# The mixers of a second transformer block: TensorE's order written in the source, long convolution and linear attention interleaved with column projections

## The chip, the cores and the metric

One core of one Trainium2 chip runs the whole program, a network of several blocks, in one launch. The metric is the device time of an execution in microseconds (us). TensorE (PE) multiplies matrices, VectorE (DVE) and ScalarE (ACT) work element by element, SyncE (SP) issues transfers; each engine takes its instructions from a queue of its own, in order, and instructions of different engines wait for each other by semaphores.

## What is computed

The change concerns the four mixers of the second block. The input of the block is normalised, multiplied by one wide matrix `w_in`, and its columns feed the mixers; their outputs are normalised by group and multiplied by `w_out`:

```python
h = rms_norm_2(x, norm_g[l, 0])
q, k, v, g, lr, u_f, u_h, u_s = jnp.split(h @ w_in[l], split_at, axis=-1)
y_a = gla_mixer(q, k, v, g, lr, gla_gk_w[l], gla_gk_b[l], gla_norm_g[l])
y_b = rms_norm_2(fnet_mixer(u_f), grp_norm_g[l, 0])
y_c = rms_norm_2(hyena_mixer(u_h, hy_conv_w[l], filt, hy_skip[l]), grp_norm_g[l, 1])
y_d = rms_norm_2(shortconv_mixer(u_s, sc_conv_w[l]), grp_norm_g[l, 2])
mix = jnp.concatenate([y_a, y_b, y_c, y_d], axis=-1)
x = x + mix @ w_out[l]
```

`gla_mixer` is a linear attention with gates, worked in chunks of 64 tokens, forward and backward, then normalised by head and multiplied by silu(g). `fnet_mixer` is the real part of a Fourier transform over tokens and channels. `hyena_mixer` is two long convolutions by a Fourier transform of twice the length (`z = x1 * long_conv(v)`, then `x2 * long_conv(z)`) after a convolution of width 3. `shortconv_mixer` is `b * short_conv(c * h)`. There are 256 tokens, a model width of 2048, and each mixer gives 512 channels.

## The kernel before

A projection by columns (`colsA`, helper `formA`, L191) makes 128 columns of `h @ w_in` for all 256 tokens: the weights come as two raw tiles of 128 x 1024, ACT rounds each to whi (L187), DVE subtracts to wlo (L188), and PE runs, for each of 16 slices of the model width, the pair L207 (whi, 512 columns: high and low part of the tokens) and L208 (wlo, 256 columns). So a column group is 32 matmuls into one accumulator `acc`, of which there are two. `fold` adds the two halves of the accumulator: a copy on ACT (L212) and an addition on DVE (L213). The rounded weights have two buffers, the raw ones four. `formB` (L215, matmuls L224 to L226) makes V with the tokens as rows.

`hyena` takes 12 column groups. The first six were already made at the end of the block before (`s.first`, in the PSUM tiles acc, acc, iv, iv, ch, yb); each is folded into the one tile "pu" (L1734 to L1737) and convolved (`conv3`, L1700 on ACT, L1701 and L1702 on DVE). Then follow transposes (L1758), the transforms (L1765), products on DVE (L1770 to L1776), the transforms back (L1782) and the products with skip and gate (L1783, L1784), twice. `group_rms` (L1709) squares four tiles on ACT (L1715, one buffer "cat"), adds them up over the channels by a matmul with ones (L1716), takes root (L960, ACT) and reciprocal (L961, DVE) and writes the normalised tiles `MIX`. `gla` makes the low-rank gate input, Q, K, V and the gate g, then for two directions and two pairs of heads the gates (L1876 to L1886: a small matmul, abs, exp and ln on ACT, a scan on DVE), the scaled Q and K (L1893 to L1905), transposes (L1909), masked scores (L1919 to L1924) and states (L1933 to L1937), at last the outputs (L1944, L1953) and the norm by head (L1957 to L1964). `fnet` has four column groups and for each two small transforms (L1803, L1808); `shortconv` has 12 column groups.

Up to the end of the block ahead (`l1`) PE's order is the order of the source, by `manual_schedule`. The second block stands outside of that: on PE too a scheduler sets the order, by its priorities and its own cost model, and mixes column groups between the steps of the mixers. The quoted lines are those that call it:

```python
        with tc.manual_schedule(engines={ET.PE}):
            next(head, None)
            s.l0()
            s.mem_again()
            s.nsplit = 2
            s.l1()
            s.nsplit = 1
        s.block2()
```

Of the kernel before, what the change touches and what calls it, by code (L numbers as in the profile page):

```python
# [13 lines left out]
AF = mybir.ActivationFunctionType  # L14
# [7 lines left out]
P = 128  # L22
# [114 lines left out]
class _K:  # L137
    hs = [slice(0, 64), slice(64, 128)]
# [1569 lines left out]

    def group_rms(s, Y, gname, gi, f0):  # L1709

        nc = s.nc
# [13 lines left out]

    def hyena(s):
        nc, I = s.nc, s.I
        outs = []
        for b, tag in enumerate(("S0", "S1", "BK")):
            o = s.T(tag, [P, 4, 256])  # L1730
            for i in range(4):
                acc = s.colsA(2080 + 512 * b + 128 * i) if 4 * b + i > 5 else s.first[4 * b + i]
                u = s.T("pu", [P, 258])
                nc.vector.memset(u[:, 0:1], 0.0)  # L1734
                nc.vector.memset(u[:, 257:258], 0.0)
                s.fold(u[:, 1:257], acc)
                nc.vector.tensor_tensor(u[:, 1:257], u[:, 1:257], s.R, MUL)  # L1737
                s.conv3(o[:, i], u, "hcv", 4 * b + i, 12)
            outs.append(o)
        Z, X1, X2 = outs  # L1740
# [7 lines left out]
        for o in range(2):  # L1748
# [6 lines left out]
            for t in range(2):  # L1755
                ps = s.PS("sc", (P, 4, 128))
                for i in range(4):
                    nc.tensor.transpose(ps[:, i], Z[:, i, t * 128:(t + 1) * 128], s.ident)  # L1758
                nc.scalar.copy(zt[t], ps.rearrange("p i c -> p (i c)"))
            Yf = []  # L1760
            for m in range(2):
# [15 lines left out]
                Yf.append((yr, yi))  # L1777
            Ys = [Yf[0][0], Yf[1][0], Yf[0][1], Yf[1][1]]
            for i in range(4):
# [4 lines left out]
                nc.vector.tensor_tensor(Z[:, i], Z[:, i], (X1 if o == 0 else X2)[:, i], MUL)  # L1784
        s.group_rms(Z, "gpn", 4, 8)

    def fnet(s):
        nc, I = s.nc, s.I
        fc = s.T("pw", [P, 256])
# [4 lines left out]
        Y = s.T("S1", [P, 4, 256])  # L1794
        for g in range(4):
            acc = s.colsA(1568 + 128 * g)
            u = s.T("pu", [P, 256])
# [6 lines left out]
            nc.scalar.copy(xc, ps)  # L1804
            po = s.PS("ch")
# [4 lines left out]
        s.group_rms(Y, "gpn", 0, 4)  # L1810

    def shortconv(s):
        nc = s.nc
        Y = s.T("S0", [P, 4, 256])
        for i in range(4):
            acc = s.colsA(3616 + 512 + 128 * i)
            c = s.T("aa", [P, 256])
# [3 lines left out]
            acc = s.colsA(3616 + 1024 + 128 * i)  # L1821
            u = s.T("pu", [P, 258])
# [5 lines left out]
            acc = s.colsA(3616 + 128 * i)  # L1828
            b = s.T("kk", [P, 256])
# [3 lines left out]
        s.group_rms(Y, "gpn", 8, 12)  # L1833

    def gla(s):
        nc, I = s.nc, s.I
        hs = [slice(0, 64), slice(64, 128)]
        acc = s.colsA(1536, 32)
        lr = s.T("pu", [32, 256])
        s.fold(lr, acc)  # L1840
        nc.vector.tensor_tensor(lr, lr, s.R[0:32], MUL)
# [4 lines left out]
        Q, K = s.T("r0", [P, 2, 256]), s.T("k0", [P, 2, 256])  # L1846
        for t in range(2):
            acc = s.colsA(128 * t)
            s.fold(Q[:, t], acc)
            nc.vector.scalar_tensor_tensor(Q[:, t], Q[:, t], 0.125, s.R, MUL, MUL)  # L1850
            acc = s.colsA(256 + 128 * t)
            s.fold(K[:, t], acc)
            nc.vector.tensor_tensor(K[:, t], K[:, t], s.R, MUL)
        accs = [s.PS("acc"), s.PS("acc")]
# [4 lines left out]
        SG = s.T("BK", [P, 4, 256])  # L1859
        for h in range(4):  # L1860
            acc = s.colsA(1024 + 128 * h)
            s.fold(SG[:, h], acc)
            nc.vector.tensor_tensor(SG[:, h], SG[:, h], s.R, MUL)
            th = s.T("cat", [P, 256])
            nc.scalar.activation(th, SG[:, h], AF.Tanh, scale=0.5)
            nc.vector.scalar_tensor_tensor(SG[:, h], th, 1.0, SG[:, h], ADD, MUL)
# [4 lines left out]
        qe_tags = {(0, 0): "vs", (0, 1): "YS", (1, 0): "ss", (1, 1): "w65"}  # L1871
        for d in range(2):
            rv = (lambda a: a) if d == 0 else (lambda a: a[:, ::-1])
            for t in range(2):
                ps = s.PS("ch")
                nc.tensor.matmul(ps[:, 0:256], gw[:, d, t * 128:(t + 1) * 128], lr, start=True, stop=True)  # L1876
                z = s.T("wi", [P, 256])
                nc.vector.tensor_scalar(z, ps[:, 0:256], s.par("gkb", 2 * d + t), None, ADD)
                e = s.T("aa", [P, 256])
                nc.scalar.activation(e, z, AF.Abs)  # L1880
# [27 lines left out]
                for m in range(2):  # L1908
                    nc.tensor.transpose(ps[:, m, 0:128], x[:, m * 128:(m + 1) * 128], s.ident)  # L1909
# [201 lines left out]
```

## Time and profile before

| | us |
|---|---|
| three executions | 3622.12, 3622.71, 3631.28 |
| median | 3622.71 |
| the profiled execution | 3619.33 |
| its span in the trace | 3616.1 |
| mixers' stage in it, on PE | 2268.7 to 2563.0 |

The profile is of one execution. Its span goes from the first to the last instruction; a group of instructions is named by its line, engine and operation, and "out<-in" gives the tiles. A time in brackets behind an instruction is how long its engine stood idle ahead of it, and behind the arrow stands what ended that. "PEclk" is the clock that PE was granted, 1.00 for 2.4 GHz and 0.50 for 1.2 GHz.

### The profile page before, as it was taken

Reading aid. Unit: us, or ns where it says so; the run is one execution under the profiler, and the core shown is the slowest. Engines: PE = TensorE matmul, PEld = TensorE weight load, DVE = VectorE, ACT = ScalarE, POOL = GpSimd, SP = SyncE. Lnnn points to the kernel's source line nnn. Section 1 sums busy time; section 2 is a strip of 40 time slices with the busy share of each in tenths; the row PEclk is TensorE's granted clock in tenths of the full one; section 3 lists DMA queues with packets and bytes.
Section 4 is the critical chain, followed back from the end, with each engine's and each line's share of the span. In section 5 each row is a group of like instructions: output and inputs, shape, how many; then the busy total and the mean of one; then the engine's idle time right before and its main releaser. Section 6 shows DMA issues by size and latency. Waiting matters only on the chain.

```text
span 3616.1 us, 57152 instructions
## 1 busy us (share of the span) xinstructions
PE 3481.6 (96%) x22385; PEld 2678.9 (74%) x22385; DVE 2253.2 (62%) x4345; ACT 1624.8 (45%) x2845; POOL 83.4 (2%) x168
## 2 busy tenths in 40 slices
PE   6999999999999999999999999999999999999998
PEld 4576666666666666678788887777888888888886
DVE  4253666677776677853656667766654566666544
ACT  3244343444444444432546555364444544444433
POOL 1000000000000000100000000000000000000000
PEclk9999999999999999999999999998999999999999
DMA  9986443334343344353444457554665566666655
GB/s 303 308 268 184 132 118 115 115 118 133 106 131 119 112 124 120 117 161 106 137 122 125 138 179 209 134 136 118 184 181 164 180 190 189 191 189 191 201 190 162
DMA packets 655656, 578.61 MB, mean 160 GB/s; under 512 B 24891, under 2 KB 498415, under 8 KB 655386
## 3 DMA queue, kind: packets, MB, share of 16 engines
q1 hardware_dynamic: 627008, 538.86, 50.1%
q10 hardware_dynamic: 24474, 29.09, 2.4%
q0 software_dynamic: 3904, 7.01, 0.7%
q8 instruction: 175, 2.87, 0.3%
q14 instruction: 95, 0.78, 0.1%
HBM read 547.32 MB, written 27.56 MB: 159 GB/s over the span
## 4 chain that ended last, share of the span: by engine, by line
issue 58%; PE 17%; DVE 3%; ACT 2%; DMA 1%; POOL 0%; ACTq 0%; POOLq 0%; SPq 0%; DVEq 0%
PE acc L486 3%; PE iv L708 3%; PE acc L487 2%; PE acc L488 2%; DMA raw<-ev_w_in 1%; PE acc L369 1%; PE ch L776 1%; PE ch L780 1%; PE sc L692 1%; PE ch L770 1%; PE yb L784 1%; PE yb L785 0%; ACT whi L187 0%; DVE S L701 0%; DMA catT<-sg 0%
## 5 line engine op out<-in xcount | busy, mean ns | idle before, releaser
L188 DVE TENSOR_TENSOR wlo<-raw,whi 128x512 fp32r<-128x512 f32 (+1 forms) x1022 | 942.8, 937 | 789.1 <-ACT whi L187 784.5
L187 ACT CAST whi<-raw 128x512 fp32r<-128x512 f32 (+1 forms) x1022 | 819.1, 821 | 1029.7 <-PE acc L207 205.3
L207 PE MATMUL acc<-A,whi 128*128 128x512 f32 x1488 | 529.8, 397 | 0.8 <-ACT whi L187 0.8
L208 PE MATMUL acc<-A,wlo 128*128 128x256 f32 x1488 | 423.5, 285 | 0.9 <-DVE wlo L188 0.9
L486 PE MATMUL acc<-A,whi 128*128 128x512 f32 x768 | 359.1, 468 | 22.5 <-ACT ev L497 13.8
L207 PEld LDWEIGHTS acc<-A,whi 128*128 128x128 f32 x1488 | 277.9, 187 | 64.3 <-ACT whi L187 1.4
L487 PE MATMUL acc<-B,whi 128*128 128x512 f32 x768 | 303.2, 395 | 0.0
L488 PE MATMUL acc<-A,wlo 128*128 128x512 f32 x768 | 301.8, 393 | 0.0
L208 PEld LDWEIGHTS acc<-A,wlo 128*128 128x128 f32 x1488 | 280.3, 188 | 5.3 <-DVE wlo L188 2.1
L207 PE MATMUL iv<-A,whi 128*128 128x512 f32 x736 | 257.5, 391 | 0.0
L208 PE MATMUL iv<-A,wlo 128*128 128x256 f32 x736 | 206.5, 281 | 1.2 <-DVE wlo L188 1.1
L486 PEld LDWEIGHTS acc<-A,whi 128*128 128x128 f32 x768 | 145.7, 190 | 81.4 <-issue 31.8
L488 PEld LDWEIGHTS acc<-A,wlo 128*128 128x128 f32 x768 | 144.8, 188 | 33.4
L487 PEld LDWEIGHTS acc<-B,whi 128*128 128x128 f32 x768 | 146.2, 190 | 21.9 <-issue 9.6
L207 PEld LDWEIGHTS iv<-A,whi 128*128 128x128 f32 x736 | 137.7, 187 | 30.2
L208 PEld LDWEIGHTS iv<-A,wlo 128*128 128x128 f32 x736 | 139.1, 189 | 2.3 <-DVE wlo L188 2.3
L720 DVE TENSOR_TENSOR x<-iv,k 128x256 f16<-128x256 f32 x160 | 67.6, 422 | 89.9 <-PE iv L708 88.0
L777 ACT COPY UV<-ch 64x128 f32<-64x128 f32 x128 | 33.4, 261 | 183.7 <-PE ch L776 176.3
L708 PEld LDWEIGHTS <-at 64*64 64x64 f16 x1536 | 40.3, 108 | 92.9 <-issue 75.5
L708 PEld LDWEIGHTS <-y 64*64 64x64 f16 x1536 | 39.8, 107 | 82.9 <-issue 50.5
L737 DVE TENSOR_TENSOR t<-iv,t 128x256 f16<-128x256 f32 x128 | 54.2, 423 | 49.5 <-PE iv L708 47.2
L776 PE MATMUL ch<-R,Y 128*128 128x128 f32 x256 | 63.1, 329 | 14.4 <-DVE R L772 14.2
(1540 smaller groups left out, 7147.8 us busy)
## 6 DMA issues: line engine op xcount, KB each, us to landing
raw<-w_gate_up SPq DMA_DIRECT2D x176, 512.0 KB, 4.8
raw<-mod_w SPq DMA_DIRECT2D x128, 512.0 KB, 3.9
raw<-ev_w_in SPq DMA_DIRECT2D x100, 512.0 KB, 4.4
raw<-w_down SPq DMA_DIRECT2D x88, 512.0 KB, 4.8
raw<-od_w_in SPq DMA_DIRECT2D x80, 512.0 KB, 3.7
raw<-w_in SPq DMA_DIRECT2D x80, 512.0 KB, 4.0
raw<-w_xkv SPq DMA_DIRECT2D x64, 512.0 KB, 6.8
A<-mod_w SPq DMA_DIRECT2D x64, 512.0 KB, 6.6
```

Of the source, the lines that this page charges most:

```text
L187: nc.scalar.copy(hi[:, q], raw[:, q])
L188: nc.vector.tensor_sub(lo[:, q], raw[:, q], hi[:, q].bitcast(F32))
L207: s.nc.tensor.matmul(acc, hi, x.rearrange("p a t -> p (a t)"), start=start, stop=False)
L208: s.nc.tensor.matmul(acc[:, 0:256], lo, x[:, 0], start=False, stop=stop)
L369: nc.tensor.matmul(acc[32 * q:32 * q + 32], s.SC[:, 2 * k:2 * k + 32], pair[q // 2][:, q % 2], start=k < 4, stop=k >= 12, tile_position=(0 ...
L486: s.nc.tensor.matmul(acc, hi[:, k], hX[kx], start=kx == 0, stop=False)
L487: s.nc.tensor.matmul(acc, hi[:, k], lX[kx], start=False, stop=False)
L488: s.nc.tensor.matmul(acc, lo[:, k], hX[kx], start=False, stop=kx == 15)
L708: nc.tensor.matmul(ps[hs[h], c], l(hs[h], c), r(hs[h], c), start=True, stop=True)
L720: tt(X16, px, b4(s.lv[d][l]), MUL)
L737: tt(T16 if l < 5 else T32, pt, T16, ADD)
L776: nc.tensor.matmul(pr[:, 128:256], fl(Y32[:, b:b + 2]), R1, start=True, stop=True)
```

## The change

`block2` is cut in two. Part 1, `mixers`, now runs inside the `manual_schedule` of PE, so PE's order there is the order of the source; DVE, ACT and the queues are still ordered by the scheduler. Part 2 (output projection, cross attention, feed-forward) stays outside.

`colsG` is the column projection as a generator: it yields after every second slice, two pairs L207+L208, a half-step. `hyena` and `gla` become generators that yield numbers at the points where they would wait; `between(main, fill)` runs that many half-steps of the filler at each. The outputs of the six ready column groups are emitted first, then groups 6 to 8 whole. Hyena's filler is groups 9 to 11 and then all projections of the attention (`gla_in`, in the order lr, q, k, g, V). The attention's filler is the column groups of `fnet`, each with the transform of the group before it at its half-steps 2 and 4, then those of `shortconv`. What is left of a filler is drained. The group norms of hyena and fnet are one block each. Many tiles have other names, so that what runs at the same time has buffers of its own: Q, K and V in m0 to m3, the gate in "op", fnet's in "rs", "ss", "ks", "BK" and "AT", shortconv's in "TW", "T32", "ev" and "w2".

```diff
+    def colsG(s, c0, done, m=128):
+        acc = s.PS("acc")[0:m]
+        W = s.I["w_in_2"][0]
+        for k0 in (0, 8):
+            hi, lo = s.wload(W[k0 * P:(k0 + 8) * P, c0:c0 + m].rearrange("(k p) c -> p k c", p=P), 8, m)
+            for k in range(8):
+                s.pair(acc, hi[:, k], lo[:, k], s.H[k0 + k], k0 + k == 0, k0 + k == 15)
+                if k % 2 and k0 + k < 15:
+                    yield
+        done(acc)
+        yield
+    @staticmethod
+    def between(main, fill):
+        for n in main:
+            for _ in range(n):
+                next(fill, None)
...
+    def hy_out(s, q, acc):
+        nc = s.nc
+        u = s.T("pu", [P, 258])
+        nc.vector.memset(u[:, 0:1], 0.0)
+        nc.vector.memset(u[:, 257:258], 0.0)
+        s.fold(u[:, 1:257], acc)
+        nc.vector.tensor_tensor(u[:, 1:257], u[:, 1:257], s.R, MUL)
+        s.conv3(s.hy[q // 4][:, q % 4], u, "hcv", q, 12)
+    def hy_cols(s, qs):
+        for q in qs:
+            yield from s.colsG(2080 + 128 * q, lambda acc: s.hy_out(q, acc))
     def hyena(s):
...
+        Z, X1, X2 = s.hy
...
                 nc.scalar.copy(zt[t], ps.rearrange("p i c -> p (i c)"))
+                yield 2
...
                 Yf.append((yr, yi))
+                yield 5 + m
...
                 nc.vector.tensor_tensor(Z[:, i], Z[:, i], (X1 if o == 0 else X2)[:, i], MUL)
+                yield 1
+            yield 2
         s.group_rms(Z, "gpn", 4, 8)
...
+        us = []
+        def done(acc):
+            u = s.T(("rs", "ss")[len(us) % 2], [P, 256])
             s.fold(u, acc)
             nc.vector.tensor_tensor(u, u, s.R, MUL)
-            xc = s.T("wi", [P, 2, 256])
+            us.append(u)
+        def mix(g):
+            u = us[g]
+            xc = s.T("ks", [P, 2, 256])
             ps = s.PS("sc", (P, 2, 256))
             for t in range(2):
                 nc.tensor.matmul(ps[:, t], u[:, t * 128:(t + 1) * 128], fc, start=True, stop=True)
             nc.scalar.copy(xc, ps)
+            yield
             po = s.PS("ch")
             for n in range(4):
                 q, t = n // 2, n % 2
                 nc.tensor.matmul(po[:, 0:256], xc[:, t, q * 128:(q + 1) * 128], ft[q][:, t], start=n == 0, stop=n == 3)
             nc.scalar.copy(Y[:, g], po[:, 0:256])
-        s.group_rms(Y, "gpn", 0, 4)
+        def cols(g):
+            x = s.colsG(1568 + 128 * g, done) if g < 4 else iter(())
+            for i, _ in enumerate(x):
+                if g > 0 and i in (2, 4):
+                    next(s.mx, None)
+                yield
+            if g < 4:
+                s.mx = mix(g)
+        for g in range(4):
+            yield from cols(g)
+        s.fn_last = s.mx
+        s.fn_Y = Y
...
+        for i in range(4):
+            for n, _ in enumerate(s.colsG(3616 + 512 + 128 * i, f0)):
+                if i == 0 and n in (2, 4):
+                    next(s.fn_last, None)
+                yield
+            for n, _ in enumerate(s.colsG(3616 + 1024 + 128 * i, lambda acc: f1(acc, i))):
+                if i == 0 and n == 1:
+                    s.group_rms(s.fn_Y, "gpn", 0, 4)
+                yield
+            yield from s.colsG(3616 + 128 * i, lambda acc: f2(acc, i))
+        s.sc_Y = Y
...
+        for t in range(2):
+            yield from s.colsG(128 * t, lambda acc: f_q(acc, t))
+            yield from s.colsG(256 + 128 * t, lambda acc: f_k(acc, t))
...
+        for h in range(4):
+            yield from s.colsG(1024 + 128 * h, lambda acc: f_g(acc, h))
         accs = [s.PS("acc"), s.PS("acc")]
-        s.drain(s.formB(I["w_in_2"][0], 512, s.toks(s.H), accs))
-        V = [s.T(tag, [P, 512]) for tag in ("rs", "ks")]
...
+        nx = gate(*par[0])
+        yield 6
+        for i, (d, t) in enumerate(par):
+            sx = scaled(d, t, nx)
+            if i < 3:
+                nx = gate(*par[i + 1])
+            yield 7
+            yield from chunks(d, t, *sx)
         O = s.T("S0", [P, 4, 256])
...
             nc.scalar.copy(O[:, hd], po[:, 0:256])
+            yield 1
...
             s.split(s.MIX, hd, O[:, hd])
+            yield 2
...
+    def mixers(s):
+        s.MIX = s.big("B")
+        s.hy = [s.T(tag, [P, 4, 256]) for tag in ("S0", "S1", "BK")]
+        for q in range(6):
+            s.hy_out(q, s.first[q])
+        s.drain(s.hy_cols((6, 7, 8)))
+        def fill():
+            yield from s.hy_cols((9, 10, 11))
+            yield from s.gla_in()
+        x = fill()
+        s.between(s.hyena(), x)
+        s.drain(x)
+        def fill():
+            yield from s.fnet()
+            yield from s.shortconv()
+        x = fill()
+        s.between(s.gla(), x)
+        s.drain(x)
+        s.group_rms(s.sc_Y, "gpn", 8, 12)
+    def block2(s, part):
         nc, I = s.nc, s.I
-        s.MIX = s.big("B")
-        s.hyena()
-        s.gla()
-        s.fnet()
-        s.shortconv()
+        if part == 1:
+            s.mixers()
+            return
         s.proj_add(I["w_out_2"][0], s.MIX, ng=16)
         s.xdump("x3")
         s.cross()
@@ -2089,7 +2205,8 @@
             s.nsplit = 2
             s.l1()
             s.nsplit = 1
-        s.block2()
+            s.block2(1)
+        s.block2(2)
 _INS = list(_SHAPES)
```

Lines move: in the changed kernel L1736 is the L1716 of before, L1779 is L1758, L1787 is L1765, L1833 and L1839 are L1803 and L1808, L1863 to L1864 and L1825 are products with the row of factors after a fold, L1955 to L1961 are the gates L1880 to L1886, L1971 to L1985 the scaled Q and K of L1893 to L1912, L1934 the copy L1858, L1992 is L1909, L2052 is L1959, and L2055 to L2057 are L1962 to L1964.

Where the instructions stand now is shown at three places, as the built programs have them. A number behind a name tells tiles apart.

The first is PE at the beginning of the stage, before: `yb_23837` is the last of the six ready groups, `acc_23956` group 6, `S0` holds the first convolved outputs and `iv` takes the transform.

```order
L208 MATMUL yb_23837<-A7_23267,wlo_23841 128x256
L207 MATMUL acc_23956<-A0_23260,whi_23959 128x512
...
L208 MATMUL acc_24010<-A7_23267,wlo_24036 128x256
L1758 MATMUL sc_24299<-k128_65,S0_23900 128x128 x3
...
L1765 MATMUL iv_24311<-wi_24297,TW_24281 128x512
L1765 MATMUL iv_24311<-aa_24298,TW_24281 128x512
...
L1765 MATMUL iv_24328<-wi_24297,TW_24281 128x512
L207 MATMUL acc_24065<-A0_23260,whi_24068 128x512
```

The same place after:

```order
L208 MATMUL yb_23837<-A7_23267,wlo_23841 128x256
L207 MATMUL acc_23956<-A0_23260,whi_23959 128x512
...
L208 MATMUL acc_23956<-A7_23267,wlo_23982 128x256
L207 MATMUL acc_24010<-A0_23260,whi_24013 128x512
...
L208 MATMUL acc_24010<-A7_23267,wlo_24036 128x256
L207 MATMUL acc_24064<-A0_23260,whi_24067 128x512
...
L208 MATMUL acc_24064<-A7_23267,wlo_24090 128x256
L1779 MATMUL sc_24136<-k128_65,S0_23899 128x128 x4
L207 MATMUL acc_24142<-A0_23260,whi_24145 128x512
```

Before, the first transposes follow group 7 and the transforms follow them; after, the whole of group 8 (`acc_24064`, the third group on two accumulators) stands between group 7 and the first transposes, and two half-steps of group 9 (`acc_24142`) between the first and the second set of them.

The second place is ACT at the first column group of the Fourier mixer. Before (`acc_25452` is that group, `pu_25497` its fold):

```order
L1880 ACTIVATE aa_25224<-wi_25222 128x256
L1881 ACTIVATE aa_25224<-aa_25224 128x256
L1882 ACT_TABLE_LOAD
L1882 ACTIVATE aa_25224<-aa_25224 128x256
L1910 COPY rn_25178<-sc_25179 128x256
L212 COPY pu_25497<-acc_25452 128x256
L187 CAST whi_25537<-raw_25535 128x1024
```

After (`acc_25104` is that group, `rs_25177` its fold, the operand of L1833):

```order
L1971 ACTIVATE vs_25141<-kk_25095 128x256
L1985 ACTIVATE sm4_25155<-kk_25095 128x4
L187 CAST whi_25211<-raw_25209 128x1024
L1976 ACTIVATE kp_25146<-tb_25144 128x256
L1977 ACTIVATE kp_25146<-tb_25144 128x256
L1955 ACTIVATE aa_25161<-wi_25159 128x256
L212 COPY rs_25177<-acc_25104 128x256
L1956 ACTIVATE aa_25161<-aa_25161 128x256
L1957 ACT_TABLE_LOAD
L1957 ACTIVATE aa_25161<-aa_25161 128x256
L1982 ACT_TABLE_LOAD
L1982 ACTIVATE tb_25151<-tb_25151 128x256
```

and DVE after, where L1958 takes the result of the second L1957 and L1983 that of L1982:

```order
L1979 TENSOR_TENSOR kp_25146<-kp_25146,m1_24480 128x256
L1981 TENSOR_TENSOR tb_25151<-kk_25095 128x256
L1958 SCALAR_TENSOR_TENSOR wi_25159<-wi_25159,aa_25161 128x256
L213 TENSOR_TENSOR rs_25177<-rs_25177,acc_25104 128x256
L1983 TENSOR_TENSOR tb_25151<-tb_25151,m1_24480 128x256
L1959 TENSOR_SCALAR wi_25159<-wi_25159 128x256
L1825 TENSOR_TENSOR rs_25177<-rs_25177,inv_23861 128x256
```

On ACT the fold's copy L212 now stands in the middle of the second gate's functions, and on DVE the product L1825 that makes L1833's operand stands behind two results of ACT that come after further table loads. On PE, L1833 stands 12 matmuls behind the group that it works on.

The third place is DVE at the end of the attention's norm. Before:

```order
L961 RECIPROCAL rn_25401<-rn_25401 128x256
L188 TENSOR_TENSOR wlo_25636<-raw_25633,whi_25635 128x1024
L1962 TENSOR_TENSOR S0_25356<-S0_25356,rn_25401 128x256
L1963 SCALAR_TENSOR_TENSOR S0_25356<-S0_25356,PT_103,BK_24877 128x256
L1964 TENSOR_SCALAR S0_25356<-S0_25356 128x256
L188 TENSOR_TENSOR wlo_25658<-raw_25655,whi_25657 128x1024
L1009 TENSOR_TENSOR B0_23892<-S0_25356,B0_23892 128x256
L961 RECIPROCAL rn_25413<-rn_25413 128x256
L213 TENSOR_TENSOR pu_25617<-pu_25617,acc_25572 128x256
L1962 TENSOR_TENSOR S0_25356<-S0_25356,rn_25413 128x256
```

After (`wlo_25923` and `wlo_25945` are the two halves of one short-convolution group):

```order
L961 RECIPROCAL rn_25840<-rn_25840 128x256
L2055 TENSOR_TENSOR S0_25767<-S0_25767,rn_25840 128x256
L188 TENSOR_TENSOR wlo_25923<-raw_25920,whi_25922 128x1024
L2056 SCALAR_TENSOR_TENSOR S0_25767<-S0_25767,PT_103,op_24728 128x256
L961 RECIPROCAL rn_25860<-rn_25860 128x256
...
L2055 TENSOR_TENSOR S0_25767<-S0_25767,rn_25860 128x256
...
L961 RECIPROCAL rn_25886<-rn_25886 128x256
...
L2055 TENSOR_TENSOR S0_25767<-S0_25767,rn_25886 128x256
...
L961 RECIPROCAL rn_25911<-rn_25911 128x256
L1009 TENSOR_TENSOR B1_23892<-S0_25767,B1_23892 128x256
L2055 TENSOR_TENSOR S0_25767<-S0_25767,rn_25911 128x256
L188 TENSOR_TENSOR wlo_25945<-raw_25942,whi_25944 128x1024
```

Before, a cast L188 stood between the reciprocals L961 two times out of three; after, three reciprocals and 15 other rows stand between the casts of the two halves.

## Rows read from the trace of the kernel before

**Rows 1.** The page, part 1: busy time, share of the span, instructions.

```profile
PE 3481.6 (96%) x22385; PEld 2678.9 (74%) x22385; DVE 2253.2 (62%) x4345; ACT 1624.8 (45%) x2845; POOL 83.4 (2%) x168
```

**Rows 2.** Windows of the stage: length, busy us of each engine (instructions), PEclk, DMA share, GB/s.

```profile
2268.70:2563.00 294.30, 279.57 (x1467) 220.97 (x1466) 198.31 (x365) 134.39 (x218) 0.00 (x0) 0.95 0.50 133
...
2369.00:2395.00 26.00, 24.56 (x102) 18.15 (x101) 16.34 (x25) 19.41 (x28) 0.00 (x0) 1.00 0.58 160
...
2430.00:2440.00 10.00, 5.32 (x41) 3.30 (x40) 6.66 (x21) 7.51 (x12) 0.00 (x0) 0.78 0.07 21
2440.00:2450.00 10.00, 7.83 (x33) 5.32 (x33) 8.66 (x22) 2.31 (x7) 0.00 (x0) 0.50 0.19 45
2450.00:2460.00 10.00, 10.00 (x51) 7.93 (x51) 1.75 (x7) 1.33 (x3) 0.00 (x0) 0.53 0.40 112
...
2499.00:2563.00 64.00, 62.54 (x358) 54.38 (x357) 45.57 (x70) 30.08 (x43) 0.00 (x0) 1.00 0.71 187
```

**Rows 3.** Waits of PE in the stage: us in total, times, longest.

```profile
PE ch L1808 <- ACT rn L960: 1.5, 1, 1.5
...
PE yb L1933 <- DVE pv L1937: 0.4, 1, 0.4
```

**Rows 4.** Timeline of PE at the start: start, us, instruction [idle before <-releaser].

```profile
2278.43 0.39 PE L207 MATMUL acc<-A,whi 128*128 128x512 f32 x1
...
2279.12 0.39 PE L207 MATMUL acc<-A,whi 128*128 128x512 f32 x1
...
2279.81 0.82 PE L1758 MATMUL sc<-k,S 128*128 128x128 f32 x6
2283.17 0.44 PE L1758 MATMUL sc<-k,S 128*128 128x128 f32 x2 [2.54 <-DVE S L1702]
...
2289.41 1.02 PE L1765 MATMUL iv<-wi,TW 128*128 128x512 f32 x2
2290.27 1.02 PE L1765 MATMUL iv<-aa,TW 128*128 128x512 f32 x2
...
2292.91 0.79 PE L207 MATMUL acc<-A,whi 128*128 128x512 f32 x1
```

**Rows 5.** Timeline of ACT there: the folds of outputs 4 and 5.

```profile
2283.20 0.38 ACT L212 COPY pu<-ch 128x256 f32<-128x256 f32 x1 [1.85 <-DVE S L1702]
...
2286.17 0.38 ACT L212 COPY pu<-yb 128x256 f32<-128x256 f32 x1 [1.13 <-DVE S L1702]
```

**Rows 6.** Groups by line and form in the stage: busy us, mean ns | idle before.

```profile
L188 DVE TENSOR_TENSOR wlo<-raw,whi 128x1024 fp32r<-128x1024 f32 x68 | 83.1, 1223 | 53.0 <-ACT whi L187 53.0
L187 ACT CAST whi<-raw 128x1024 fp32r<-128x1024 f32 x68 | 71.5, 1052 | 97.3 <-PE acc L207 73.9 <-issue 19.3 <-PE acc L226 1.6
...
L961 DVE RECIPROCAL rn<-rn 128x256 f32<-128x256 f32 x6 | 10.5, 1749 | 8.8 <-ACT rn L960 8.8
...
L1882 ACT ACT_TABLE_LOAD x4 | 5.1, 1283 | 0.1
...
L1715 ACT ACTIVATE cat<-S 128x256 f32<-128x256 f32 x9 | 3.8, 419 | 4.6 <-PE ch L1716 4.6
...
L213 DVE TENSOR_TENSOR BK<-BK,acc 128x256 f32<-128x256 f32 x4 | 1.7, 414 | 0.0
```

**Rows 7.** Waits of PE in two stretches far ahead, 37 to 44 and 357 to 365.

```profile
PE acc L207 <- DVE m L990: 5.7, 1, 5.7
...
PE acc L486 <- ACT ev L497: 5.6, 1, 5.6
```

**Rows 8.** Windows in and after these two waits.

```profile
39.40:49.60 10.20, 6.53 (x21) 3.54 (x21) 3.66 (x5) 3.22 (x5) 0.00 (x0) 0.50 1.01 286
...
360.30:367.10 6.80, 3.46 (x8) 2.79 (x9) 4.62 (x9) 4.40 (x7) 0.00 (x0) 0.50 0.48 161
```

**Rows 9.** Timeline of PE at the gates of the attention.

```profile
2435.70 0.72 PE L1919 MATMUL iv<-kp 64*64 64x64 f32 x16 [1.96 <-DVE kp L1901]
...
2439.92 0.69 PE L1909 MATMUL sc<-k,tb 128*128 128x128 f32 x2 [2.69 <-DVE tb L1905]
```

More of the change, by code (lines that the diff above doesn't have):

```diff
@@ L1793, in fnet @@
             nc.sync.dma_start(ft[i], I["kft"][i].rearrange("(t p) k -> p t k", p=P))
[L1794 to L1797, printed above, removed]
+        Y = s.T("BK", [P, 4, 256])
+        us = []
+        def done(acc):
+            u = s.T(("rs", "ss")[len(us) % 2], [P, 256])
             s.fold(u, acc)
             nc.vector.tensor_tensor(u, u, s.R, MUL)
-            xc = s.T("wi", [P, 2, 256])
+            us.append(u)
+        def mix(g):
+            u = us[g]
+            xc = s.T("ks", [P, 2, 256])
             ps = s.PS("sc", (P, 2, 256))
@@ L1809, in fnet, with f0 @@
             nc.scalar.copy(Y[:, g], po[:, 0:256])
-        s.group_rms(Y, "gpn", 0, 4)
+        def cols(g):
[10 more added lines that the diff above has]
+        s.fn_Y = Y
     def shortconv(s):
         nc = s.nc
[L1814 to L1817, printed above, removed]
+        Y = s.T("TW", [P, 4, 256])
+        cs = {}
+        def f0(acc):
+            c = cs[0] = s.T("T32", [P, 256])
             s.fold(c, acc)
@@ L1820, in shortconv, with f1 @@
             nc.vector.tensor_tensor(c, c, s.R, MUL)
-            acc = s.colsA(3616 + 1024 + 128 * i)
-            u = s.T("pu", [P, 258])
+        def f1(acc, i):
+            c = cs[0]
+            u = s.T("ev", [P, 258])
             nc.vector.memset(u[:, 0:1], 0.0)
@@ L1827, in shortconv, with f2 @@
             s.conv3(Y[:, i], u, "scv", i, 4)
-            acc = s.colsA(3616 + 128 * i)
-            b = s.T("kk", [P, 256])
+        def f2(acc, i):
+            b = s.T("w2", [P, 256])
             s.fold(b, acc)
@@ L1832, in shortconv, with gla_in, f_lr @@
             nc.vector.tensor_tensor(Y[:, i], Y[:, i], s.R, MUL)
-        s.group_rms(Y, "gpn", 8, 12)
-    def gla(s):
-        nc, I = s.nc, s.I
[L1837 to L1841, printed above, removed]
+        for i in range(4):
[9 more added lines that the diff above has]
+        s.sc_Y = Y
+    def gla_in(s):
+        nc, I = s.nc, s.I
+        lr = s.T("Y321", [32, 256])
+        def f_lr(acc):
+            s.fold(lr, acc)
+            nc.vector.tensor_tensor(lr, lr, s.R[0:32], MUL)
+        yield from s.colsG(1536, f_lr, 32)
         gw = s.T("pw", [32, 2, 256])
@@ new lines, in gla, with gate @@
+        qe_tags = {(0, 0): "vs", (0, 1): "YS", (1, 0): "pu", (1, 1): "w65"}
+        rv = lambda d, a: a if d == 0 else a[:, ::-1]
+        par = [(d, t) for d in range(2) for t in range(2)]
+        def gate(d, t):
+            ps = s.PS("ch")
+            nc.tensor.matmul(ps[:, 0:256], gw[:, d, t * 128:(t + 1) * 128], lr, start=True, stop=True)
+            z = s.T("wi", [P, 256])
+            nc.vector.tensor_scalar(z, ps[:, 0:256], s.par("gkb", 2 * d + t), None, ADD)
+            e = s.T("aa", [P, 256])
+            nc.scalar.activation(e, z, AF.Abs)
+            nc.scalar.activation(e, e, AF.Exp, scale=-1.0)
+            nc.scalar.activation(e, e, AF.Ln, bias=1.0)
+            nc.vector.scalar_tensor_tensor(z, z, 0.0, e, MIN, SUB)
+            nc.vector.tensor_scalar(z, z, 1.0 / 16, None, MUL)
+            b = s.T("kk", [P, 256])
+            nc.vector.tensor_tensor_scan(rv(d, b), s.rm[:, 0:256], rv(d, z), 0.0, MUL, ADD)
+            return b
```

167 lines of the change are left out of this document (74 added, 93 removed).

## Prediction

> **What bounds the kernel now.** I read the page first: TensorE (PE) is busy 96% of the span [rows 1]. A change that alters only order can then win or lose no more than what PE now loses in the stretch it touches. That is the mixers' stage of the second block: its first column group that is not already fixed by hand begins at 2268.7 us, the output projection at 2563.0, so 294.3 us. Everything ahead of the first transposes of the long convolution and everything after the stage has the same order on PE, VectorE (DVE) and ScalarE (ACT) in both programs.
>
> Next the stretches of the stage [rows 2]. Where PE only runs column groups it loses little: 62.54 us busy of 64 in the last one. The loss is in one place, 2430 to 2460, where the gates of the linear attention are worked: PE is busy 23.15 of 30 us and its clock falls to 0.50, the lower level. The waits [rows 3] say what ends the idle time: DVE and ACT results of small chains, no transfer. VectorE has room all the while, 198 of the stage's 294 us busy [rows 2]. So the question is: which waits does the written order remove, and which queue head blocks PE in its place?
>
> The unit of account is the pair of matmuls L207+L208 (512 and 256 columns): they follow each other every 0.346 us (2278.43 to 2279.12 is two of them, start to start) [rows 4], so a column group of 16 takes 5.54 us, and one half-step of the new filler (two pairs) 0.69 us.
>
> **The change, part by part.** PE executes the same matmuls: 496 pairs, 96 of L224 to L226, the same small ones. ACT, DVE and the queues issue as many instructions as before; transfers that move are the small tables (kfc, kft) and none is waited for in the stage now, so I cost them at nothing; the cover is more than 5 us of pairs behind each issue, and one late small load would cost about a pair's wait, under 2 us.
>
> *1. The start: +7.0 us.* Before, PE goes from group 7 to the first transposes (L1758) at 2279.81 and to the transforms (L1765), and starts group 8 at 2292.91 [rows 4]: 13.1 us, with a wait of 2.54 and the lower clock in it. At full rate that work (8 transposes in 1.1, 14 transform passes at 0.43 by the rows at 2289.41 and 2290.27, one L1782) takes 7.5, so 5.6 us are lost there now. After, group 8 stands ahead of the transposes. There are two accumulators, so it waits until group 6 has been folded, and that fold shares the one tile "pu" with the outputs 4, 5 and 6, which go one after another: the folds of outputs 4 and 5 begin at 2283.20 and 2286.17, a cycle of 2.97 us [rows 5]. Two cycles after 2283.20 comes group 6's fold, 0.38 on ACT and 0.41 on DVE [rows 6]: it ends at 2289.93. PE is idle from 2279.8 to about 2290.0: 10.2 us. The clock then is low for a while. Two other gaps show by how much: after 5.7 us of idle time [rows 7] PE was busy 6.53 us at 0.50, after 5.6 us 3.46 us [rows 8]; half of such busy time is lost, so 1.7 to 3.3, and I take 2.4. 10.2 + 2.4 - 5.6 = +7.0; bounds +5 (nothing lost to the clock) and +9.
>
> *2. End of the long convolution: +2.3.* The group norm's four matmuls now stand in one block with no pair between, and the squares share one buffer: each later one waits for a square of 0.42 [rows 6] and two hand-overs. Three such steps of some 0.6 and the first 0.4: 2.3; bounds 0 (squares early) and 3.
>
> *3. The projections of the attention: +1.3.* Before, PE idles 1.44 us of the 26 from 2369 to 2395 [rows 2], where table loads on ACT stand ahead of the casts. After, no gate runs beside L224, so that goes. New: the second accumulator of V waits for the fold of the last gate group behind a cast of 1.05 on ACT and 1.22 on DVE [rows 6]: about 2.7 with the copies. Bounds -1.4 and +2.
>
> *4. The attention, before's losses: -16.3.* A wait of 1.96 us ends at 2435.70, one of 2.69 at 2439.92 [rows 9], and from the first on PE is at the lower clock until nearly 2460 (0.50, then 0.53 in the mean) [rows 2]. Of the 23.15 busy us some 4.3 were at full speed, 18.9 at half speed (9.4 of work), so 13.7 us of work took 30. In the written order pairs stand between all steps, and this goes.
>
> *5. The attention, new waits: +13.8.* The Fourier mix (L1833) of column group 0 now stands 12 matmuls behind that group, and its operand passes the queues of ACT and DVE behind the second gate's chain (the order shown above). From the first gate's matmul ACT and DVE need: bias 0.48, abs, exp, a table load of 1.283, ln (0.42 each) [rows 6], a cast 1.05, another load, exp, the decays, a cast 1.05 that waits for PE, two exps, abs, the fold's copy, exp, load, ln, load, exp, and DVE's last product, add and multiply. Added up with 0.08 overlap per hand-over that is 12.6 us. PE has in that time 44 half-pairs at 0.173 and a small matmul: 7.7. The wait is 4.9, and at the lower clock after such a gap another 1.7. The mix of group 3 by the same count 1.9; the state matmuls and masks 2.5 (the rows of before show single waits of 0.4 to 2.7 [rows 3, 9]; none at one end, 5 at the other); the Fourier group norm in one block 2.8. Sum 13.8; bounds 4 and 20.
>
> By the Trainium skill ("ScalarE: Activation LUTs", "What ACT_TABLE_LOAD costs") a switch of tables costs the load of some 1283 ns and a drain of some 1380 ns. The trace has the load, but 0.0 to 0.1 us of idle time in all before four of them [rows 6], so the drain does not show and I leave it out; by the page's figure the mix's wait would be 2 x 1.4 us longer, an estimate that would put this term at 16.6.
>
> *6. The tail: +9.5, and -1.9 and -1.5 of before.* The attention's last norm has one PSUM bank ("ch") and one tile "rn", so its fourth matmul waits for the root of the third, that for the second's product. DVE does these in a row (order above): from the cast wlo of the first half of a short-convolution group to the second product 2.6 us and the root 0.48, against about 1.0 of pairs: 2.1 idle. From there to the cast of the second half DVE has 15 rows, two reciprocals of 1.749 and one cast of 1.22 among them [rows 6]: 9.5, less overlap 8.3. PE has 0.5 + 3.0 us of work. It waits 4.8. With 2.6 for the clock after it: 9.5; bounds 2 and 13. Before has the same four reciprocals, but casts between them, and lost 1.5 there (L1808 behind the root) [rows 3] and 0.4 beside it. The end of the stage loses 1.46 now [rows 2], which goes since the last groups run bare.
>
> *7.* 11 switches between forms of matmul fewer, about 0.06 each: -0.7.
>
> **Sum:** 7.0 + 2.3 + 1.3 - 16.3 + 13.8 + 9.5 - 1.9 - 1.5 - 0.7 = +13.5. The profiled execution took 3619.3 us (3616.1 of span), 3.4 under the median of 3622.7; by its own time the changed kernel takes 3632.8, by the median 3636.
>
> **Rivals.** *Not slower (a): the queue heads are on time.* Terms 5 and 6 hang on one thing: that DVE and ACT, which hold back the gates, are as far behind PE as my count says. For it: DVE has a third of the stage free [rows 2], and the leads that the order gives are 2 to 8 us of PE's work. Against it: ACT's chain is serial and has the table loads in it [rows 6]. It decides at the operand of the first mix: if that is ready within the 12 matmuls (2.1 us) ahead of it, nothing waits. Then 5 falls by 11 and 6 by 9.5, 13.5 - 20.5 = -7.0; if the squares of the two group norms are early too, their 5.1 and the clock's 2.4 go as well, -14.5. I put it at 3612 (3608 to 3616). *(b): half of it.* One of the two, 5 or 6, does not come: about +3, 3626 (3620 to 3632). *(c) the clock.* Several gaps of 2 to 5 us follow each other in terms 5 and 6; before, two gaps of 2 and 2.7 us [rows 9] were enough for 24 us at the lower level [rows 2]. If the attention falls into that again, 9 us (what half speed took there) or more come on top: +24, 3647 (3643 to 3654). That the order were not what the source says is excluded: the built program shows it, on PE only; DVE and ACT keep an order that is not written by hand.
>
> **How the numbers follow.** Forecast 0.48, range 3628 to 3644; (a) 0.20; (b) 0.20; (c) 0.12. 0.3% is 10.9 us, about what a measurement of this kernel can tell from no change. Slower by more: 0.33 of the forecast's 0.48 and (c), 0.45. Faster by more: six tenths of (a), 0.12. The rest 0.43: 0.15 of the forecast, 0.08 of (a), all of (b). Forecast and (c) end on one side, (a) on the other, so the range takes from 3612 to 3650 and leaves out half of (a), a third of (c) and the ends, about 0.2.
>
> **What would show it.** In the trace after: an idle time of PE of about 10 us ahead of an L207 into acc, released by the fold of group 6 on DVE (term 1); L1833 waiting 4 to 5 us for DVE's rs (term 5); L1736 in steps behind ACT's squares (2); near the end L208 waiting for wlo behind a row of reciprocals (6). No half clock at the gates, but after those gaps. I am wrong if PE starts group 8 before 2287, if L1833 does not wait, or if the stage ends before 2563.

## The result, and the profile after

Ten executions of each kernel: before 3631.66 us in the median (3617.37 to 3636.33), after 3647.32 (3639.28 to 3656.64). The ratio of the means is 1.0054, 95% interval 1.0043 to 1.0066: slower by 0.5%, some 20 us (the medians differ by 15.7). The profiled execution took 3653.31 us, its span is 3651.5, and the mixers' stage in it lasts from 2269.6 to 2588.7: 319.1 us against 294.3, +24.8.

The waits of PE in the stage after (us in total, times, longest):

```profile
PE acc L207 <- DVE pu L213: 10.1, 1, 10.1
PE sc L1833 <- DVE rs L1825: 5.4, 2, 4.9
PE acc L208 <- DVE wlo L188: 3.4, 2, 3.0
PE ch L1736 <- ACT cat L1735: 3.0, 6, 0.5
PE sc L1833 <- DVE ss L1825: 2.0, 1, 2.0
PE ch L2052 <- ACT rn L960: 2.0, 1, 2.0
PE acc L224 <- DVE op L213: 2.0, 1, 2.0
PE yb L2016 <- DVE sq L2020: 1.2, 1, 1.2
PE yb L2016 <- DVE sq L2018: 1.0, 1, 1.0
PE ch L1805 <- DVE S L1806: 0.7, 2, 0.5
```

Of the waits of before that [rows 3, 9] show one kind is left, and it is longer: L2016 is the state matmul L1933 of before, which waits until DVE has read the tile yb (L2020 is the L1937 of before), 0.4 us there and 1.2 and 1.0 here. The others stand at other places, the longest of them at the start. The same stage in windows (busy us of each engine, then PEclk), the whole first:

```profile
2269.60:2588.70 319.10, 288.17 (x1467) 230.56 (x1466) 199.89 (x363) 135.87 (x218) 0.00 (x0) 0.91 0.46 122
...
2279.20:2289.30 10.10, 1.69 (x10) 1.22 (x8) 7.22 (x17) 3.41 (x7) 0.00 (x0) 0.68 0.58 152
2289.30:2299.20 9.90, 8.19 (x32) 7.08 (x33) 5.67 (x17) 2.81 (x5) 0.00 (x0) 0.63 0.01 2
...
2359.70:2363.60 3.90, 2.38 (x11) 1.15 (x9) 1.78 (x3) 1.28 (x4) 0.00 (x0) 1.00 0.41 108
...
2402.70:2428.40 25.70, 23.74 (x98) 18.91 (x97) 10.98 (x11) 9.68 (x11) 0.00 (x0) 0.93 0.59 161
...
2434.10:2448.70 14.60, 9.73 (x41) 8.08 (x41) 8.51 (x17) 9.38 (x17) 0.00 (x0) 0.77 0.30 82
...
2479.70:2489.30 9.60, 9.50 (x69) 6.92 (x67) 6.58 (x18) 5.33 (x12) 0.00 (x0) 1.00 0.28 73
2489.30:2493.20 3.90, 2.38 (x7) 1.16 (x8) 2.27 (x5) 1.60 (x4) 0.00 (x0) 1.00 0.10 13
...
2500.90:2532.10 31.20, 29.00 (x109) 23.68 (x106) 9.32 (x26) 5.46 (x11) 0.00 (x0) 0.56 0.31 85
2532.10:2548.00 15.90, 10.90 (x49) 8.79 (x48) 14.93 (x24) 6.71 (x13) 0.00 (x0) 0.89 0.13 34
```

The row to look at is 2500.90 to 2532.10. PE is busy 29.0 of 31.2 us, so by the share of busy time nothing is wrong there; but the granted clock is 0.56 in the mean. The timeline of PE shows what comes ahead of it:

```profile
2502.94 0.43 PE L2016 MATMUL yb<-m,op 64*64 64x128 f32 x4 [1.01 <-DVE sq L2018]
2503.30 0.50 PE L207 MATMUL acc<-A,whi 128*128 128x512 f32 x1
...
2505.46 0.69 PE L2016 MATMUL yb<-m,op 64*64 64x128 f32 x4 [1.19 <-DVE sq L2020]
2506.08 0.80 PE L207 MATMUL acc<-A,whi 128*128 128x512 f32 x1
...
2507.53 0.63 PE L2036 MATMUL ch<-S,m 128*128 128x128 f32 x2
```

Two waits of about 1 us at the states (L2016), with 1.3 us of work between them; in the second, at 2504.8, the clock falls to the lower level. From there the matmuls take 1.6 times as long (an L2016 of four 0.69 in place of 0.43, an L207 0.80 in place of 0.50), for 27.3 us, all through the four outputs of the attention (L2036 and L2045). That is what stood at 2435 to 2460 before [rows 2], at another place. State steps with one half-step of pairs each and no wait ran at 1.00 earlier (the row 2479.70 to 2489.30).

The stage's +24.8 is more than the runs' difference. The rest of the profiled pair differs too, in code that is the same in both, the gate and up projections of the feed-forward, without a wait and at the upper clock in both; the first row is of before, the second of after:

```profile
3000.00:3100.00 100.00, 100.00 (x579) 88.15 (x578) 67.76 (x100) 48.35 (x72) 0.00 (x0) 1.00 0.67 190
```

```profile
3000.00:3100.00 100.00, 100.00 (x568) 86.74 (x567) 66.92 (x99) 46.91 (x70) 0.00 (x0) 1.00 0.65 187
```

579 matmuls against 568 in 100 us. What follows the stage took 1052.9 us before and 1062.6 after, 9.7 more, in single executions: of the ten experiments below seven show 578 or 579 there and three 567 to 569, with edits that do not touch that part. So the time of one execution says little here, and I read the experiments by the length of the stage in their traces.

### The profile page after: what moved, and what is told of

Same layout as the page of the kernel before. It is cut to its first block, busy times and chain, and to the rows that moved or that the text cites. A ratio compares the mean times of both kernels' runs of the same rounds, so it can differ in the third digit from the quotient of the medians.

```text
span 3651.5 us, 57144 instructions
## 1 busy us (share of the span) xinstructions
PE 3495.8 (96%) x22385; PEld 2689.8 (74%) x22385; DVE 2254.2 (62%) x4345; ACT 1622.8 (44%) x2845; POOL 83.2 (2%) x168
## 4 chain that ended last, share of the span: by engine, by line
issue 60%; PE 30%; DVE 4%; ACT 3%; DMA 3%; ACTq 0%; POOL 0%; SPq 0%; POOLq 0%; DVEq 0%
PE acc L486 4%; PE acc L487 4%; PE acc L488 4%; PE iv L708 3%; PE acc L369 2%; PE acc L207 1%; DMA raw<-ev_w_in 1%; PE ch L776 1%; PE sc L692 1%; PE ch L780 1%; PE yb L1685 1%; PE ch L770 1%; PE yb L784 1%; PE acc L208 1%; PE yb L785 1%
## 5 line engine op out<-in xcount | busy, mean ns | idle before, releaser
L188 DVE TENSOR_TENSOR wlo<-raw,whi 128x512 fp32r<-128x512 f32 (+1 forms) x1022 | 942.8, 937 | 814.1 <-ACT whi L187 808.2
L207 PE MATMUL acc<-A,whi 128*128 128x512 f32 x1488 | 546.6, 408 | 10.1 <-DVE pu L213 10.1
L208 PE MATMUL acc<-A,wlo 128*128 128x256 f32 x1488 | 424.5, 285 | 3.9 <-DVE wlo L188 3.8
L486 PE MATMUL acc<-A,whi 128*128 128x512 f32 x768 | 359.3, 468 | 22.4 <-ACT ev L497 13.9
L207 PEld LDWEIGHTS acc<-A,whi 128*128 128x128 f32 x1488 | 282.1, 190 | 81.9 <-issue 14.9
L208 PEld LDWEIGHTS acc<-A,wlo 128*128 128x128 f32 x1488 | 284.5, 191 | 7.9 <-DVE wlo L188 5.5
L207 PE MATMUL iv<-A,whi 128*128 128x512 f32 x736 | 262.2, 399 | 0.0
L208 PE MATMUL iv<-A,wlo 128*128 128x256 f32 x736 | 207.4, 282 | 1.4 <-DVE wlo L188 1.4
L207 PEld LDWEIGHTS iv<-A,whi 128*128 128x128 f32 x736 | 138.4, 188 | 34.3
L487 PEld LDWEIGHTS acc<-B,whi 128*128 128x128 f32 x768 | 146.4, 191 | 21.8 <-issue 9.6
L208 PEld LDWEIGHTS iv<-A,wlo 128*128 128x128 f32 x736 | 139.3, 189 | 2.2 <-DVE wlo L188 2.2
```

Source lines behind the costliest of these rows:

```text
L188: nc.vector.tensor_sub(lo[:, q], raw[:, q], hi[:, q].bitcast(F32))
L207: s.nc.tensor.matmul(acc, hi, x.rearrange("p a t -> p (a t)"), start=start, stop=False)
L208: s.nc.tensor.matmul(acc[:, 0:256], lo, x[:, 0], start=False, stop=stop)
L486: s.nc.tensor.matmul(acc, hi[:, k], hX[kx], start=kx == 0, stop=False)
L487: s.nc.tensor.matmul(acc, hi[:, k], lX[kx], start=False, stop=False)
```

## The experiments

All but the last two start from the changed kernel, with a stage of 319.1 us.

**The start.** The edit moves two outputs behind groups 6 to 8; PE's order stays.

```diff
-        for q in range(6):
+        for q in range(4):
             s.hy_out(q, s.first[q])
         s.drain(s.hy_cols((6, 7, 8)))
+        for q in (4, 5):
+            s.hy_out(q, s.first[q])
```

> Undoes the cause named for the start: the outputs 4 and 5 of the long convolution (needed only a hundred matmuls later) are emitted after groups 6 to 8, PE's order stays the same word for word. My theory (group 8 waits for the fold of group 6, which stands behind the outputs 4 and 5 on the one tile pu): group 6's fold follows output 3, two cycles of 2.97 us earlier, so the idle time of 10.1 us ahead of group 8 falls to about 4.2, the low clock after it from about 2.6 us lost to 1.5, and the stage from 319.1 to about 312. Rival (PE waits there for weights or for a transfer): the idle time stays near 10 us and the stage near 319.

PE's waits from 2268 to 2300:

```profile
PE acc L207 <- DVE pu L213: 4.2, 1, 4.2
```

The stage took 312.0 us. Both numbers are those of the theory: 5.9 of the 10.1 us were two cycles of the tile "pu" for outputs that nobody needed yet. The 4.2 that are left wait for the same tile.

**The states before the outputs.**

```diff
-                yield 1
+                yield 3 if (d, t) == (1, 1) else 1
```

> Three half-steps of pairs in place of one behind each state matmul of the last direction and head pair, nothing else. After the two waits of 1.0 and 1.2 us there PE ran 27.3 us at the lower clock. Theory A (these waits bring the clock down): both waits go, no long stretch at the lower clock, and the stage falls by 2.2 + 9 to 12, to about 306. Theory B (the output step behind it, many small matmuls with one half-step of pairs between, does it): both waits go, but the lower clock comes again in the output step; the stage falls by about 2, to 317.

The outputs now run from 2507.7 to 2520; a window around them:

```profile
2500.00:2530.00 30.00, 26.54 (x155) 21.36 (x154) 17.23 (x36) 10.75 (x21) 0.00 (x0) 1.00 0.44 122
```

The two waits are gone, no long low stretch comes, and the stage took 309.6, 9.5 less. One other wait stands ahead of the outputs now, with 3 us of nearly only pairs behind it, and the clock stayed up:

```profile
2504.44 0.39 PE L208 MATMUL acc<-A,wlo 128*128 128x256 f32 x1 [1.24 <-DVE wlo L188]
```

The stage is short of 306 by that wait and because the tail lost more: L208 waits there for wlo 4.8 us once, against 3.0; the norm steps now stand at other places of the column groups, which was not tried apart. So the outputs by themselves run at the upper clock if no wait comes just ahead of them. The edit does two things at once, though: it takes the waits away, and it puts more pairs ahead of the outputs. That the waits are what brings the clock down rests also on the row 2479.70 above and on the sixth experiment.

**The outputs.**

```diff
             nc.scalar.copy(O[:, hd], po[:, 0:256])
-            yield 1
+            yield 4
```

> Four half-steps of pairs in place of one behind each of the four outputs of the attention. Theory A (the waits in the states bring the clock down): it falls again at about the same place, 2504.8, and the stage stays within 3 us of 319. Theory B (the sparse output step does it, or keeps it down): the low stretch is gone or 7 us at most, and the stage falls by 8 to 12, to about 309.

```profile
2503.90:2514.10 10.20, 9.50 (x34) 7.82 (x35) 3.05 (x10) 1.26 (x3) 0.00 (x0) 0.50 0.30 87
2514.10:2530.00 15.90, 15.90 (x99) 13.71 (x98) 6.13 (x9) 4.66 (x9) 0.00 (x0) 1.00 0.39 99
```

The clock falls at the same place, 2503.9, in the second of the same two waits, but comes back after 10.2 us where it took 27.3. Stage 314.4, 4.7 less: the tail took part of the gain, with waits of 2.9 and 3.3 us for 2.0 and 3.0. So neither theory alone: the waits bring it down, and the sparse outputs keep it down. With pairs between them it comes back in the middle of the same step.

**The tail.**

```diff
             s.split(s.MIX, hd, O[:, hd])
-            yield 2
+            yield 8
```

> Eight half-steps of pairs in place of two behind each of the four norm steps of the attention, so that DVE's four reciprocals have 5.5 us of pairs each. My theory (the tail's waits are the reciprocals and products in DVE's queue): the waits of 2.0 us for the root and 3.0 us for the cast go, and the low clock of 3.4 us after them: the stage falls by 6 to 9, to about 311. Rival (DVE is short of time in the tail as a whole, casts included): the waits move to later groups and the stage falls by less than 2.

PE's waits from 2530 to the end of the stage:

```profile
PE acc L208 <- DVE wlo L188: 1.4, 2, 0.9
```

1.4 us in place of 5.0, and no low clock behind it. Stage 313.3, 5.8 less, just short of the 6 to 9 expected. With pairs beside the reciprocals in DVE's queue most of the tail's wait goes.

**V's accumulators.**

```diff
-        accs = [s.PS("acc"), s.PS("acc")]
+        accs = [s.PS("iv"), s.PS("iv")]
```

> V is accumulated in the two PSUM tiles iv, which are free by then, in place of the two acc, nothing else. My theory: the wait of 2.0 us of the second accumulator's first L224 for the fold of the last gate group goes, and with it the low clock of 3.4 us behind it: the stage falls from 319.1 by 2.0 + 1.7, to about 315.4. Rival (V waits for its own weights, cast behind the gate group's): the wait stays, ended by a cast.

```profile
2399.00:2426.00 27.00, 27.00 (x125) 22.08 (x124) 13.38 (x16) 13.96 (x18) 0.00 (x0) 1.00 0.68 184
...
2540.00:2548.00 8.00, 6.44 (x22) 5.55 (x23) 4.10 (x8) 1.73 (x3) 0.00 (x0) 0.57 0.51 131
```

The wait and the low clock at V are gone (first row: busy throughout, 1.00), but the stage took 318.5. Elsewhere the same waits drew more at the lower clock than in the profile after: a stretch at the convolution's norm that was not there, and one behind the tail's last wait (second row). So the mechanism is shown, the gain in time is not: a difference of some 3 us between two stages, each from one execution, settles nothing. What the clock takes differs from trace to trace where the code is the same: around the same wait of 4.9 us at L1833 PE was at the lower clock for 6.8 us in five of these traces and for 3.4 in two.

**The norms drawn apart.**

```diff
             nc.tensor.matmul(ps[:, 0:256], s.ones, sq, start=i == 0, stop=i == 3)
+            yield 2
...
-        s.group_rms(Z, "gpn", 4, 8)
+        yield from s.group_rmsG(Z, "gpn", 4, 8)
...
-                if i == 0 and n == 1:
-                    s.group_rms(s.fn_Y, "gpn", 0, 4)
+                if i == 0 and 1 <= n <= 5:
+                    next(fn, None)
```

> The four squares and matmuls of the group norms of the long convolution and of the Fourier mixer are drawn apart, with two half-steps of pairs (the convolution's) and one (the Fourier mixer's) behind each. My theory (each matmul waits for the one square buffer): the six waits of 0.5 us go and the stage falls by the 2.9 and 3.0 us that the two blocks took beyond their matmuls, to about 313.5. Rival (the squares wait for the mixers' outputs, so the block is only moved): less than 2 us.

```profile
2509.98 0.38 PE L208 MATMUL acc<-A,wlo 128*128 128x256 f32 x1 [3.56 <-DVE wlo L188]
```

```profile
2510.60:2538.00 27.40, 27.40 (x97) 22.86 (x97) 5.22 (x12) 4.00 (x9) 0.00 (x0) 0.50 0.27 77
```

The six waits for squares went, and so did those of L2016. But the Fourier norm's multiplications now stand ahead of a cast on DVE: one wait of 3.56 us for wlo, and behind it again 27.4 us at 0.50 in the outputs. Stage 319.4. The gain was given back in full, by one wait at the place where it costs most. This also answers the question above a second time: another wait than L2016's, the same low stretch.

**The Fourier transforms later.** Three tiles for the folds, and

```diff
-                if g > 0 and i in (2, 4):
-                    next(s.mx, None)
+                if g > 1 and i in (2, 4):
+                    next(mx[g - 2], None)
```

> The small transforms of the Fourier mixer's column group stand two column groups behind it in place of one (three tiles for the folded groups in place of two). My theory (L1833 waits because its operand passes ACT and DVE behind the second gate's chain, some 5 us later than PE comes to it): the waits of 4.9, 2.0 and 0.5 us go, and the low clock behind the first, 6.8 us: the stage falls by 7.4 + 2.5, to about 309. Rival (PE only arrives sooner at the gates' next step and waits there): the waits of L2001 or L1992 for DVE come in their place and the stage falls by less than 4.

```profile
PE sc L1991 <- DVE tb L1982: 3.9, 1, 3.9
```

Here the rival holds. The waits for the folded groups are gone, and the first transposes of K (the L1992 of the changed kernel) wait 3.9 us for DVE's tb, the end of the same chain of gates; L1909, the same transposes, waited for the same tile before, 2.69 us [rows 9]. The waits at the gates and the mixes are less in total, but the low stretch there grew from 6.8 to 13.7 us. Stage 319.5. The wait of 4.9 us was not the transform's own: the chain of ACT and DVE is longer than the pairs written beside it, and whatever comes first on PE behind it pays, here with less filler behind the wait.

**All of it together**, with two tiles for the outputs (`s.T(("pu", "ev")[q % 2], [P, 258])`) and two half-steps behind each output of the attention.

> All of it together: outputs 4 and 5 late, two tiles for the outputs of the long convolution, three half-steps behind the last state matmuls, two behind each output and eight behind each norm step of the attention, V in iv, the norms drawn apart, the Fourier transforms two groups behind. If the parts add up, 319.1 - 7.1 - 5 (the second tile) - 9.5 - 5.8 - 3.7 - 5.9 - 9.9: a stage of 272 to 280, 14 to 22 us under the kernel before, ratio about 0.995. If the waits only move from one place to the next (the chains of ACT and DVE bound the stage), it stays over 290 and the ratio within 0.999 to 1.003.

Stage 288.8, time 3618.96 in the median of ten against 3623.79, ratio 0.9987 (0.9973 to 1.0001). At the gates 3.85 us of waiting and 17 us at the lower clock remain (3.9 and 13.7 in the run before this one), and a wait of 3.4 for wlo behind the Fourier norm. The parts do not add up, by those two.

**The gates' lead, then the Fourier norm late.** The last two start from that kernel:

```diff
-            yield 7
+            yield 13 if i == 0 else 7
```

> The kernel with all parts together, and thirteen half-steps in place of seven between the scaled Q and K of the first direction and head pair and their transposes (L1997 there). My theory (what is left at the gates is the first chain of ACT and DVE, 3.85 us longer than the pairs beside it, and the 17 us at the lower clock behind that one wait): the wait of 3.85 goes and so does the low stretch, and the stage falls from 288.8 by 3.9 + 7 to about 278. Rival (the low clock there comes of the small matmuls between the pairs): the wait goes, 10 us or more at the lower clock stay, the stage falls by 4 to 5.

The wait of the transposes at the gates went, and of the 17 us at the lower clock 3.4 are left, but the stage took 288.1, neither the 278 of the theory nor what the rival says. PE's waits from 2400 to 2490, the two longest:

```profile
PE ch L1739 <- ACT cat L1738: 4.8, 1, 4.8
PE acc L208 <- DVE wlo L188: 3.2, 1, 3.2
```

The second stands at the gates, where there was none for wlo before:

```profile
2424.56 0.58 PE L208 MATMUL acc<-A,wlo 128*128 128x256 f32 x1 [3.22 <-DVE wlo L188]
```

DVE makes that cast behind the same chain, right after its product tb and the scan. So the wait only went from the transposes to a pair, from 3.85 to 3.2 us; what was gained is the clock, as 3 us of nothing but pairs follow it. The first is new: the last of the Fourier norm's four matmuls waits for its square, and 10.2 us at the lower clock come with it. With six half-steps spent earlier, the norm now meets the masks of a later gate: the square is written into the one tile "cat", through which DVE also takes four mask products (L2010 and L2011), and ACT writes it at 2471.92, when DVE has read the last of them.

The second edit puts that norm into the last short-convolution group:

```diff
-            if i == 0:
+            if i == 3:
                 fn = s.group_rmsG(s.fn_Y, "gpn", 0, 4)
...
-                if i == 0 and 1 <= n <= 5:
+                if i == 3 and 1 <= n <= 5:
```

> As the one before, and the Fourier mixer's group norm in the last short-convolution group, behind the attention's norm. My theory (its 7 us on DVE stand ahead of a cast now, a wait of 3.4 us and 3.4 us at the lower clock): the stage falls by another 3.4 + 1.5, to about 273, 21 us under the kernel before: ratio 0.994 to 0.996. Rival (DVE is the next bound, the wait comes back at the last groups): stage 277 or more, ratio 0.996 to 0.998.

```profile
2268.80:2551.00 282.20, 270.15 (x1467) 216.49 (x1466) 194.78 (x354) 133.36 (x215) 0.00 (x0) 0.99 0.50 136
```

```profile
PE acc L208 <- DVE wlo L188: 8.3, 7, 3.2
```

The wait of 4.8 us is gone. Stage 282.1 us, 12 under before and 37 under the changed kernel, clock 0.99. Time 3608.63 in the median of six runs against 3628.12: ratio 0.9948, 0.9929 to 0.9966. This version is faster than both. By the times it gains some 19 us, by the stage 12; what the other 7 are was not tried. The waits left are mainly for casts of weights on DVE (8.3 us in seven, the longest still the one at the gates), so the stage did not come to 273: it fits the rival, DVE as the next bound, though not at the last groups alone, and the ratio fits the theory.

## Why the prediction was right and wrong

The direction, most of the places and most of the sizes were right; the clock at the attention's outputs was not. Nor does the prediction's first step hold, that a change of order can win or lose no more than PE loses there now: that bounds a gain, and nothing bounds a loss. By terms, in the profiled execution after:

1. *The start, +7.0.* The wait is 10.1 us as worked out, released by DVE's fold into "pu", and the 96 matmuls of groups 6 to 8 took 29.6 us against 16.6 at the pitch of [rows 4]: 13.0 lost, less the 5.6 of before +7.4. Shown by the first experiment.
2. *The convolution's norm, +2.3.* 3.9 us for 1.0 of matmuls: +2.9.
3. *V, +1.3.* Mis-sized. The wait is 2.0 where I reckoned 2.7, but I gave no low clock behind so short a gap, and 3.4 us of it came; 25.7 us for 21.8 of work, so 3.9 where the term has 2.7 (before the 1.4 saved there is taken off).
4. *Before's losses at the gates, -16.3: the step that failed.* "In the written order pairs stand between all steps, and this goes": it goes there, and comes back behind two waits of 1.0 and 1.2 us at the outputs, which have one half-step of pairs each. The four outputs (L2036 and L2045) with their pairs take 22.7 us there, against 12.6 with the same pairs at the upper clock in the second experiment: 10 us, which the term has at nothing. With the slow matmuls ahead of them and behind I make it 12, and the second experiment gave back 9.5 in the whole stage. I had the waits (2.5 in term 5), and rival (c) had the price (9 us or more, +24 in all, 3647), but I tied it to gaps of 2 to 5 us and gave it 0.12. Half of that was wrong: two waits of about 1 us were enough, as what follows is sparse.
5. *New waits of the attention, +13.8.* L1833 waits 4.9 and 2.0 as reckoned, the Fourier norm lost 3.0, L2016 2.2 with 2.5 allowed; the clock behind the first wait took some 2.2 in place of 1.7. That 4.9 was met to a tenth is partly luck: from the first gate's matmul (2428.40, PE goes on at 2429.02) to L1833 at 2442.75 the chain took 13.7 us in place of 12.6, and PE had 8.9 us of work beside it in place of 7.7, two misses that cancel. And the cause is the whole chain of gates, not the transform's place in it, as the seventh experiment showed.
6. *The tail, +9.5.* 2.0 for the root, 3.0 for the cast (4.8 forecast) and some 2.2 for the clock: 7.2. The waits are shown by the fourth experiment.
7. *The small terms.* Before's losses went as forecast: no wait of L1839 for the root is left, and PE is busy throughout the last 40.7 us of the stage. The -0.7 for switches of form was not measured apart.

With 12 in place of nothing for the outputs, and about +1 for the other misses together, the sum of 13.5 becomes some 26; the stage has +24.8. The ratio of many runs is only some 20 us. A shorter low stretch at the outputs in other executions is not what the traces show: in three of the experiments, with the same code there, it was 27.3 us again, in a fourth 23.9. The two paces of the feed-forward, 9 to 10 us apart, are large enough to hide 5 us; it stays open. The median of 3647 lies in the range, near its upper end and outside the forecast's own 3628 to 3644.

The drain that the Trainium skill ("ScalarE: Activation LUTs", "What ACT_TABLE_LOAD costs") adds to a table load would have made L1833's wait 7.7 us by the prediction's estimate, which counts two drains. The chain that it adds up has four loads, so by the figure of the Trainium skill it should have been some 10, again an estimate. The wait was 4.9, and in the trace after ACT's next function starts 0.01 to 0.02 us behind each of the four loads (L1957 and L1982 at 2438.26 and 2439.99 among them), so that trace does not show the drain either.

## What to carry to other kernels

Writing an engine's order by hand moves the risk from the scheduler to the heads of the other queues: for each instruction placed, follow its operand through the ACT and DVE queues, whose order nobody wrote, and give it as many microseconds of filler as that chain is long. Put the densest filler where matmuls are small and sparse, and let nothing wait just ahead of them: two waits of about 1 us there cost ten. Where a wait can't be avoided, let it fall on an instruction with dense filler behind it: at the gates a wait of 3.9 us ahead of small matmuls was followed by some 15 us at the lower clock, one of 3.2 ahead of pairs by 3. Parts that each hold may give nothing alone, as the next queue head takes the gain; so read the stage's waits again after each.

## What was not expected

A wait of 1.0 us and one of 1.2, in a stretch of small matmuls, brought 27.3 us at the lower clock, while the wait of 4.9 us with four pairs soon behind it brought 6.8, some of that within the wait itself. And the feed-forward's gate and up projections have two paces, 579 or 568 matmuls in 100 us at a clock of 1.00, which alone makes 9 to 10 us between two traces. Whether the pace goes by execution or by kernel one trace of each does not tell; the ten executions of one kernel spread over 17 to 19 us, which speaks for the former. Nothing here tried it.
